# Hymba layer on one Trainium2 core: the mixer's weight splits moved into the first FFN, by way of DRAM

## The chip, the core and the metric

The kernel runs on one core of a Trainium2 chip. Times are device microseconds (us) of one execution. The engines are TensorE (PE), VectorE (DVE), ScalarE (ACT), GpSimd (POOL) and SyncE (SP), and 16 DMA engines move data between DRAM and the on-chip memory. A run's time is compared by the median of several executions; the profile is that of a further execution.

## What is computed

One decoder layer on x of 1024 tokens by D = 1024, float32, with 16 learned meta tokens put in front (T = 1040):

```python
h = h + 0.5 * swiglu(rms_norm(h), ffn1_w_in, ffn1_w_out)
u = rms_norm(h) @ w_in                      # one combined projection
o = concat(hgrn2(u[hgrn]), stick_breaking(u[sb]))
h = h + o @ w_out
h = h + 0.5 * swiglu(rms_norm(h), ffn2_w_in, ffn2_w_out)
```

The FFNs have a width of 2816. `hgrn2` is a gated linear recurrence with 4 heads of 128, `stick_breaking` an attention with 8 heads of 64, held in 4 pairs. What matters here is `w_in` (its columns 0 to 2047 are the recurrence's q, f, v and g, and 2048 and up the attention's q, k and v) and `w_out` (1024 by 1024).

## The kernel before

**Three products for one.** All float32 products are computed as three in the reduced type fp32r. A weight block w is split into a high part wh (a cast) and a low part wl = w - wh, and PE adds wh x-high, wl x-high and wh x-low. So each weight block costs one load, one cast and one subtraction before PE can use it. The FFNs do that in `operand` (cast by ACT in L277, subtraction by DVE in L279) on blocks loaded in L284. The mixer does it in `split_w` (load by SP in L141 into a tile `raw`, cast by ACT in L148, subtraction by DVE in L150), for one column of 128 outputs by 1024 inputs (`col_tile`) or one piece of `w_out` of 512 by 128.

**FFN1-in** (`fast_in`, to about 500 us) multiplies by `ffn1_w_in` in a scheme with seven products where a 2 x 2 block product has eight; a call of `quad` does one such product of 256 output columns, on weight blocks and their sums, which POOL makes in L292 from four raw blocks. The tokens are in three parts of 352, 344 and 344: the last two go through the scheme, and the first goes along as plain products (`also`). First come 3 pairs of quads without `also`, and then 8 pairs, each a gate quad and an up quad. A steady quad takes PE 21.37 us (268.46 to 289.8 in the trace), in groups of 12 matmuls. Raw blocks have 8 buffers (4 are loaded for a quad), wh and wl have 3 each. Six times in a steady quad a finished sum is taken out of PSUM by `gate` (it ends in a silu on ACT, L395, L416 or L419) or by `up` (it ends in a multiplication on DVE, L398, L424 or L428); the results go to DRAM as `act1...` by POOL's DMA queue. `between` calls `turn_x` after each quad, which turns the input x for later (L612 to L728).

**FFN1-out** (`fast_out`, about 500 to 760 us) works in steps with names; the last is A22. Its products are L592, on halved operands that ACT and DVE make in L521 and L522. In the second part of A22 the mixer's norm runs along (L210 to L211, L1454 to L1459), and at q = 5 and 7 of A22 the k and v columns of attention pair 0 (2560 and 3072) are loaded and split (`early_w`), from a pool `we`, after an eviction.

**The mixer** (about 720 to 1430 us) takes the rest of its weights from a pool `wm` with two buffers of `raw`, `wh` and `wl` each: the q column 2048 of pair 0 first, the other nine attention columns in `sb_project` within `weave`, and the 16 recurrence columns in `hgrn_fill`, one ahead of their use. The last 14 or so of these run while the attention's blocks do (`braid`, about 920 to 1210 us), between matmuls that depend on DVE and ACT (L1072, L1121 and L1208 on PE; L1187 is DVE's part of the scores and L1215 to L1223 the stick-breaking chain). Then comes the recurrence (L831 to L980) with the first half of the output projection, and the second half (`mix_out`, L1250 to L1254; eight pieces of `w_out` each from pools `wo` and `wo2`). FFN2 (from about 1390 us) has the form of FFN1.

**What sets the order.** PE's order is written out by hand (`manual_schedule` and the generators that take turns). The other engines' instructions are put in order by a scheduler, with hints such as `tc.issue_after(instruction)`. Every engine runs its own queue in order, and so does SP with the DMAs that it issues; POOL issues DMAs too. A pool's tile is given again when its last reader is done; pools that follow each other share memory, so that a new tile may have to wait for an old one of another pool.

## Time and profile before

| | |
|---|---|
| three runs | 2099.42, 2100.28, 2101.04 us (median 2100.28) |
| profiled execution | 2096.69 us, of which 2095.0 are the span from the first to the last instruction |
| granted clock of TensorE | 0.995 of full, mean |
| instructions | 32157 |
| bytes moved by DMA | 301.12 MB, mean 144 GB/s |

The profile is taken from one execution. Its page gives busy time by engine, the span in 40 slices, the DMA queues, the chain of work that ended last (followed back from the last instruction, at each step to what released it), and the costliest groups of instructions. "a<-b" after an engine and a line is the output and the inputs by the program's names; "PE x <- DVE y" in the list of waits is an idle PE that was released by DVE's y. "SPq" and "POOLq" are the queues that issue DMAs. q1 are the DMAs issued by SP, q0 those issued by POOL. The view by windows sums the busy time of each engine in a stretch of the span.

### The profile page before, as it was taken

The page shows a single profiled execution, that of the slowest core. Times are in us where ns is not written, and L with a number is a line of the kernel's source. Part 1 is how long each engine was busy: PE and PEld are TensorE (multiplying, and loading weights), DVE is VectorE, ACT ScalarE, POOL GpSimd, SP SyncE. Part 2 cuts the span into 40 slices and gives each one's busy share as a digit, 9 for nine tenths or more (in the row PEclk, how much of TensorE's full clock was granted, in tenths as well). Part 3 has the DMA queues.
Part 4 walks back from the last instruction along what each step waited for, and adds up shares of the span by engine and source line. Part 5 has one row for each costly group of instructions (what it writes and reads, how often), then busy time and mean ns, then how long its engine had stood idle before and what let it go on. Part 6 is the DMA issues. An engine that isn't in the chain of part 4 may idle for free.

```text
span 2095.0 us, 32157 instructions
## 1 busy us (share of the span) xinstructions
PE 2026.5 (97%) x11520; PEld 1830.5 (87%) x11520; DVE 1387.2 (66%) x2140; ACT 901.6 (43%) x1860; POOL 644.6 (31%) x710
## 2 busy tenths in 40 slices
PE   7999999999999999999999998998999999999998
PEld 6999999999999989988887978886788888888887
DVE  6875544545489952258878766659767676676774
ACT  8543333333465633456666514235223233234443
POOL 2475545452000002343344300112555454440000
PEclk9999999999999999999999999999999999999999
DMA  7643333325867735435454162334333233359464
GB/s 199 188 145 121 114 108 103 99 84 192 253 201 222 237 116 163 143 127 131 121 147 120 53 253 66 97 111 126 96 101 111 93 109 101 106 196 330 136 198 136
DMA packets 272566, 301.12 MB, mean 144 GB/s; under 512 B 24694, under 2 KB 199158, under 8 KB 272406
## 3 DMA queue, kind: packets, MB, share of 16 engines
q1 hardware_dynamic: 254710, 248.62, 39.0%
q0 software_dynamic: 16656, 50.44, 6.5%
q8 instruction: 91, 1.49, 0.3%
q14 instruction: 69, 0.57, 0.1%
q10 hardware_dynamic: 1040, 0.00, 0.0%
HBM read 216.42 MB, written 82.57 MB: 143 GB/s over the span
## 4 chain that ended last, share of the span: by engine, by line
PE 83%; DVE 7%; ACT 2%; issue 1%; DMA 0%; POOL 0%; SPq 0%; DVEq 0%; ACTq 0%; POOLq 0%
PE o L592 16%; PE qb L320 13%; PE qc L320 9%; PE qa L320 8%; PE qd L320 6%; PE proj L163 5%; PE proj L164 5%; PE proj L165 5%; PE o L558 4%; PE flip L1072 2%; PE lvl L841 2%; PE wo L164 1%; PE wo L163 1%; PE wo L165 1%; DVE keep L1218 1%
## 5 line engine op out<-in xcount | busy, mean ns | idle before, releaser
L320 PE MATMUL qb<-T,wh 128*128 128x344 f32 (+1 forms) x1056 | 311.7, 358 | 9.7 <-DVE u L362 5.8
L279 DVE TENSOR_TENSOR wl<-s,wh 128x512 fp32r<-128x512 f32 x176 | 202.4, 1151 | 112.7 <-ACT wh L277 110.0
L320 PEld LDWEIGHTS qb<-T,wh 128*128 128x128 f32 x1056 | 193.0, 189 | 35.2 <-ACT wh L277 7.5
L592 PE MATMUL o<-parts 128*128 128x512 f32 x924 | 209.9, 389 | 0.0
L320 PE MATMUL qa<-B,wh 128*128 128x344 f32 (+1 forms) x704 | 209.1, 361 | 0.0
L277 ACT CAST wh<-s 128x512 fp32r<-128x512 f32 x176 | 109.4, 622 | 224.6 <-PE qb L320 154.1
L163 PE MATMUL proj<-xh,wh 128*128 128x344 f32 (+2 forms) x576 | 205.5, 357 | 0.0
L592 PEld LDWEIGHTS o<-parts 128*128 128x128 f32 x924 | 173.3, 188 | 36.0
L164 PE MATMUL proj<-xh,wl 128*128 128x344 f32 (+2 forms) x576 | 199.8, 347 | 1.1 <-DVE wl L150 1.1
L165 PE MATMUL proj<-xl,wh 128*128 128x344 f32 (+2 forms) x576 | 199.0, 346 | 0.0
L279 DVE TENSOR_TENSOR wl<-raw,wh 128x512 fp32r<-128x512 f32 x172 | 153.3, 896 | 68.0 <-ACT wh L277 64.4
L277 ACT CAST wh<-raw 128x512 fp32r<-128x512 f32 x172 | 105.8, 620 | 194.7 <-PE qc L320 97.1
L320 PE MATMUL qb<-T,wl 128*128 128x344 f32 (+1 forms) x528 | 188.3, 357 | 0.0
L320 PE MATMUL qd<-X,wh 128*128 128x352 f32 x704 | 180.8, 324 | 1.2 <-DVE X L667 1.2
L592 PE MATMUL o<-t,w 128*128 128x344 f32 x924 | 148.5, 320 | 3.9 <-DVE t L522 2.2
L592 PEld LDWEIGHTS o<-t,w 128*128 128x128 f32 x924 | 145.7, 188 | 5.6 <-DVE t L522 3.3
L292 POOL TENSOR_TENSOR s<-raw 128x512 f32<-128x512 f32 x88 | 121.5, 1381 | 92.6 <-DVE wl L279 68.3
L320 PEld LDWEIGHTS qa<-B,wh 128*128 128x128 f32 x704 | 128.5, 188 | 16.0
L1218 DVE TENSOR_TENSOR_SCAN keep<-keep 128x144 f32<-128x144 f32 (+6 forms) x112 | 128.0, 1146 | 6.7 <-ACT keep L1214 4.4
L1223 POOL TENSOR_TENSOR sig<-sig,keep 128x144 f32<-128x144 f32 (+3 forms) x64 | 87.1, 1361 | 140.4 <-DVE keep L1218 91.1
L320 PE MATMUL qa<-B,wl 128*128 128x344 f32 (+1 forms) x352 | 126.0, 358 | 0.3 <-DVE wl L279 0.3
L320 PEld LDWEIGHTS qd<-X,wh 128*128 128x128 f32 x704 | 124.7, 189 | 1.4 <-DVE X L667 1.4
(331 smaller groups left out, 4530.7 us busy)
## 6 DMA issues: line engine op xcount, KB each, us to landing
raw<-in_ffn_w_in_dram SPq DMA_DIRECT2D x208, 256.0 KB, 3.1
raw<-in_ffn_w_out_dram SPq DMA_DIRECT2D x176, 256.0 KB, 4.0
raw<-in_w_in_dram SPq DMA_DIRECT2D x28, 512.0 KB, 4.2
ks<-kD SPq DMA_DIRECT2D x32, 260.0 KB, 5.2
ak<-in_ffn_w_out_dram SPq DMA_DIRECT2D x22, 256.0 KB, 5.4
v<-vD SPq DMA_DIRECT2D x8, 576.0 KB, 4.8
hT<-xD SPq DMA_DIRECT2D x8, 520.0 KB, 7.2
xD<-xts POOLq DMA_DIRECT2D x16, 256.0 KB, 2.7
```

What stands on the lines that cost most here:

```text
L163: nc.tensor.matmul(ps, wh[:, s], xs, start=k == 0, stop=False)
L164: nc.tensor.matmul(ps, wl[:, s], xs, start=False, stop=False)
L165: nc.tensor.matmul(ps, wh[:, s], xl[:, k, c0 : c0 + n], start=False, stop=k == nk - 1)
L277: nc.scalar.copy(hi, src)
L279: nc.vector.tensor_sub(lo, src, hi.bitcast(F32))
L292: op(t, x, y)
L320: nc.tensor.matmul(ps, a[:, k, :], b[:, k0 + k, :], start=start and k == 0 and i == 0, stop=k == 3 and i == 2, skip_group_check=True,)
L558: nc.tensor.matmul(ps[m], y[:, s], z, start=f == 0 and e == 0, stop=f == D_FF // P - 1 and e == 2,)
L592: nc.tensor.matmul(banks[bank][m], y[:, m * P : (m + 1) * P], z, start=start and q == 0 and e == 0, stop=q == nq - 1 and e == 2, skip_grou ...
L841: nc.tensor.matmul(ps[:, j, :], KB[:, META + c * P : META + (c + 1) * P], QA[:, c * P : (c + 1) * P], start=True, stop=True,)
L1218: nc.vector.tensor_tensor_scan(out=kv, data0=kv, data1=kv, initial=1.0 if last else keep[:, end : end + 1], op0=ALU.mult, op1=ALU.bypass,)
L1223: nc.gpsimd.tensor_mul(sig, sig, keep[:, 1 : nk + 1])
```

## The change

In FFN1-in, from the eighth quad on, each taking of a sum (`taken`) advances a generator by one block: 512 inputs by 128 outputs of a weight of the mixer. It loads the blocks in fours into 8 buffers `early`, casts a block on ACT into the first half of a tile `both` (3 buffers), subtracts on DVE into the second half, and one step later stores the tile to DRAM by SP. There are 50 blocks: the two halves of 17 columns (k, v and q of attention pair 0, and all recurrence columns but the first two) and the 16 pieces of `w_out`. For these `split_w` gets `parts`, and loads wh and wl with two DMAs, without `raw` and without work of ACT or DVE. The nine columns of the attention's other pairs and the first two recurrence columns are split as before. The loads of columns 2560 and 3072 stand at q = 1 and 3 of A22 now, with no `issue_after`. The blocks' pool `ahead` (28 KB in a partition) lies in FFN1-in's memory, and the tiles `raw` of `we`, `wo` and `wo2` are gone.

```diff
+    def split_ahead(self, pool, groups):
+        def load(views):
+            raws = []
+            for v in views:
+                t = pool.tile([P, 512], F32, tag="raw", name="early", bufs=8)
+                nc.sync.dma_start(t.rearrange("p (k f) -> p k f", k=4), v)
+                raws.append(t)
+            return raws
...
+        made = split = None
+        for block in blocks():
+            if split:
+                nc.sync.dma_start(split[0], split[1].bitcast(F32))
+            split = None
+            if made:
+                dst, src = made
+                both = pool.tile([P, 2, 512], F32R, tag="both", name="both", bufs=3)
+                nc.scalar.copy(both[:, 0], src)
+                nc.vector.tensor_sub(both[:, 1], src, both[:, 0].bitcast(F32))
+                split = dst, both
+            made = block
+            yield
...
-    def split_w(self, view):
+    def split_w(self, view, parts=None):
         nc = self.nc
         n = int(np.prod(view.shape[1:]))
+        if parts is not None:
+            got = []
+            for i, tag in enumerate(("wh", "wl")):
+                t = self.wp.tile([P, n], F32R, tag=tag, name=tag, bufs=self.w_bufs)
+                nc.sync.dma_start(t.bitcast(F32), parts[:, i])
+                got.append(t)
+            return got
...
     def col_tile(self, w, col):
-        return self.split_w(w[:, col : col + P].rearrange("(k p) f -> p k f", p=P))
+        return self.split_w(
+            w[:, col : col + P].rearrange("(k p) f -> p k f", p=P), self.parted.get(col)
+        )
...
             def gate(i, j, ps, plus):
...
+                taken(at)
...
+                        for col in [2560, 3072, 2048] + self.columns_of_heads()[2:]:
+                            t = self.parted[col] = self.dram.tile([P, 2, D], F32, name=f"win{col}")
+                            for h in range(2):
+                                pieces.append((
+                                    t[:, :, 512 * h : 512 * h + 512],
...
+                        for k0 in (4, 0):
+                            for m in range(KT):
+                                t = self.dram.tile([P, 2, 512], F32, name=f"wout{k0}{m}")
+                                self.parted[k0, m] = t
...
+                    def taken(at):
+                        if len(seen) > 6:
+                            with tc.issue_after(at.ins):
+                                next(turning[1], None)
...
-                            if q in (5, 7):
-                                col = {5: 2560, 7: 3072}[q]
-                                with tc.issue_after(self.evicted.ins):
-                                    early_w.append(self.col_tile(a["w_in"][0], col))
+                            if q in (1, 3):
+                                early_w.append(
+                                    self.col_tile(a["w_in"][0], {1: 2560, 3: 3072}[q])
+                                )
```

Compiled, PE has the same 11200 instructions in the same order, and POOL the same 715. DVE has 2156 in place of 2139, ACT 1842 in place of 1825, and SP 1076 in place of 943; these counts are of the program and hold instructions that the page's table leaves out.

More of the change, by code (lines that the diff above doesn't have):

```diff
@@ L134, in weights, with blocks @@
         self.raw_bufs, self.w_bufs, self.split_on_vector = raw, split, on_vector
-    def split_w(self, view):
+    def split_ahead(self, pool, groups):
+        nc = self.nc
+        def load(views):
[5 more added lines that the diff above has]
+            return raws
+        def blocks():
+            nxt = load(groups[0][0])
+            yield None
+            for (_, makes), after in zip(groups, groups[1:] + [((), None)]):
+                raws, nxt = nxt, load(after[0])
+                for dst, make in makes:
+                    yield dst, make(raws)
+            yield None
+            yield None
+        made = split = None
[11 more added lines that the diff above has]
+            yield
@@ new lines, in plain_groups, with quad_group, kept @@
+    def plain_groups(self, pieces):
+        return [
+            ([v for _, v in pieces[i : i + 4]],
+             [(d, lambda raws, j=j: raws[j]) for j, (d, _) in enumerate(pieces[i : i + 4])])
+            for i in range(0, len(pieces), 4)
+        ]
+    def quad_group(self, pool, w_in, col, dst):
+        nc = self.nc
+        views = [
+            w_in[512 * h : 512 * h + 512, col + P * i : col + P * i + P]
+            .rearrange("(k p) f -> p k f", p=P) for i, h in ((0, 0), (1, 0), (1, 1), (0, 1))
+        ]
+        s = {}
+        def kept(name, op, x, y):
+            t = s[name] = pool.tile([P, 512], F32, tag="sum", name="sum", bufs=3)
+            op(t, x, y)
+            return t
+        add, sub = nc.gpsimd.tensor_add, nc.gpsimd.tensor_sub
+        return views, [
+            (dst[0], lambda r: r[0]),
+            (dst[1], lambda r: r[3]),
+            (dst[4], lambda r: kept(1, add, r[1], r[2])),
+            (dst[2], lambda r: kept(2, sub, s[1], r[0])),
+            (dst[5], lambda r: r[2]),
+            (dst[3], lambda r: kept(3, sub, r[0], r[1])),
+            (dst[6], lambda r: kept(4, sub, r[3], s[2])),
+        ]
@@ L759, in project, with columns_of_heads @@
             yield 12 * n * 0.42
+    heads_plan = [(kind, h) for h in range(4) for kind in "vfqg"]
+    def columns_of_heads(self):
+        first = {"v": 1024, "f": 512, "q": 0, "g": 1536}
+        return [first[kind] + P * h for kind, h in self.heads_plan]
     def hgrn_fill(self, xh, xl, pool, dst):
         nc = self.nc
-        plan = [(kind, h) for h in range(4) for kind in "vfqg"]
-        first = {"v": 1024, "f": 512, "q": 0, "g": 1536}
+        plan, cols = self.heads_plan, self.columns_of_heads()
         def staged(n):
@@ L1409, in run @@
                     drain(steps)
-                    drain(turning[0])
+                    for x in turning:
+                        drain(x)
                 px = self.pool("xhat1", ctx=c1)
```

38 lines of the change are left out of this document (28 added, 10 removed).

## The prediction

> **What bounds the kernel now.** First the page's busy line and its chain that ended last:
>
> ```profile
> PE 2026.5 (97%) x11520; PEld 1830.5 (87%) x11520; DVE 1387.2 (66%) x2140; ACT 901.6 (43%) x1860; POOL 644.6 (31%) x710
> ...
> PE 83%; DVE 7%; ACT 2%; issue 1%; DMA 0%; POOL 0%; SPq 0%; DVEq 0%; ACTq 0%; POOLq 0%
> ```
>
> TensorE (PE) sets the time nearly everywhere; the change touches none of its instructions, so it can win only the gaps in PE and lose only by making new ones. Where the gaps are is told by the windows view, cut at the stages (columns: us, then busy us of PE, weight loads, DVE, ACT, POOL, then clock, DMA share, GB/s):
>
> ```profile
> 183.00:365.00 182.00, 182.00 (x1161) 181.84 (x1160) 89.75 (x135) 60.64 (x111) 91.32 (x98) 1.00 0.34 108
> 690.00:760.00 70.00, 66.59 (x426) 65.61 (x425) 56.51 (x123) 36.54 (x82) 6.40 (x12) 1.00 0.57 176
> 920.00:1210.00 290.00, 276.42 (x1789) 244.79 (x1788) 230.37 (x317) 181.76 (x459) 112.74 (x147) 0.99 0.41 115
> 1210.00:1330.00 120.00, 108.59 (x783) 96.60 (x782) 83.34 (x172) 37.93 (x126) 7.30 (x7) 1.00 0.43 151
> 1400.00:1520.00 120.00, 108.43 (x464) 87.02 (x463) 95.33 (x148) 49.21 (x88) 44.85 (x42) 0.96 0.35 110
> ```
>
> In FFN1-in (183 to 365) PE has no gap, and DVE, ACT and DMA are half idle or more: the new work goes there. At the end of FFN1-out (690 to 760) and in the mixer, DVE is 70 to 81% busy and PE loses 3.4, 13.6 and 11.4 us: the old work comes out of there. The waits of PE in those stretches say on whom (us in total, times, longest):
>
> ```profile
> PE o L592 <- DVE w L522: 1.7, 1, 1.7
> PE o L592 <- DVE t L522: 1.7, 1, 1.7
> ...
> PE proj L164 <- DVE wl L150: 1.1, 1, 1.1
> ...
> PE flip L1072 <- DVE wu L1187: 8.6, 16, 1.9
> PE flip L1072 <- DVE wm L1187: 2.5, 4, 1.1
> PE flip L1121 <- DVE wu L1187: 1.5, 2, 1.0
> ...
> PE flip L1072 <- DVE vm L831: 1.5, 1, 1.5
> ...
> PE wo L164 <- DVE wl L150: 1.5, 1, 1.5
> ```
>
> Only two of these (1.1 and 1.5) wait on a mixer split itself (L150). The others wait on other DVE work, which a split on the same queue may have delayed.
>
> **The change, part by part: what is removed.** The splits by line (min/median/max ns):
>
> ```profile
> L148 ACT CAST wh<-raw x44: 613/1048/1061, 714.0 to 1396.2; 128x1024 fp32r<-128x1024 f32 x28, 128x512 fp32r<-128x512 f32 x16
> L150 DVE TENSOR_TENSOR wl<-raw,wh x44: 670/1216/2858, 722.2 to 1396.9; 128x1024 fp32r<-128x1024 f32 x28, 128x512 fp32r<-128x512 f32 x16
> ```
>
> 33 of the 44 go: 17 columns of 1024 (1.05 us ACT, 1.2 us DVE each) and 16 output pieces of 512 (about 0.62 and 0.69). That is 28 us of ACT and 31 us of DVE, but it counts only where DVE is late.
>
> 1. *k and v of pair 0, end of FFN1-out.* The chain of waits runs here through DVE, and both splits lie on it:
>
> ```profile
> 713.24 3.94 DMA act<-act16T
> ...
> 722.33 1.14 DVE wl L150
> ...
> 727.66 1.14 DVE wl L150
> ```
>
> Without them the chain is 2 x 1.14 = 2.3 us shorter, out of 3.4 us of PE gaps: -2.3 (0 to -3.4). In their place four loads of 512 KB are issued about 709, ahead of that act load on SP's queue. 2 MB at the 350 GB/s derived below are 6 us; the operands behind are issued some 10 us ahead of use, so I take 0 (to +3).
>
> 2. *q of pair 0.* One wait goes, -1.1:
>
> ```profile
> 767.32 0.50 PE L164 MATMUL proj<-xh,wl 128*128 128x512 f32 x1 [1.12 <-DVE wl L150]
> 754.63 1.06 DVE L1454 SCALAR_TENSOR_TENSOR nt<-hT,gm,rs 128x344 f32<-128x344 f32 x2 [3.77 <-ACT rs L1450]
> ```
>
> The two loads now wait for tiles that the norm gives up near its last step (754.6); two of 512 KB should land some 6 us later, 6 us ahead of that matmul.
>
> 3. *14 recurrence columns, 920 to 1210.* 14 x 1.2 = 17 us leave a DVE that is busy 230 of 290, and PE waits 12.6 us on its L1187. That is 22 waits of 0.6 us each, spread over the stage, while a split falls about every 21 us; by DVE's order at most 3 or 4 of the long ones stand shortly behind one. I take -2 (0 to -5, 4 splits of 1.2).
>
> 4. *Output projection, first half (8 pieces).* One wait of 1.5 (on L831) comes directly behind a split of 0.69: -0.7 (0 to -3).
>
> 5. *Second half.* From the timeline:
>
> ```profile
> 1373.95 10.17 SPq L141 DMA_DIRECT2D raw<-in_w_out_dram  x4
> ...
> 1380.55 1.14 ACT L148 CAST wh<-raw 128x512 fp32r<-128x512 f32 x2
> 1381.73 2.00 DVE L150 TENSOR_TENSOR wl<-raw,wh 128x512 fp32r<-128x512 f32 x2
> ...
> 1383.18 0.50 PE L164 MATMUL wo<-oH,wl 128*128 128x512 f32 x1 [1.47 <-DVE wl L150]
> ```
>
> The first parts now land by themselves before 1381.7: -1.5 (nothing else is late there).
>
> 6. *FFN2's opening.* Its first raw loads were issued only here, since their tiles overlap the mixer's raw tiles:
>
> ```profile
> 1414.81 3.29 SPq L284 DMA_DIRECT2D raw<-in_ffn_w_in_dram  x6
> ...
> 1432.51 1.67 ACT L277 CAST wh<-raw 128x512 fp32r<-128x512 f32 x3
> 1433.34 1.28 DVE L279 TENSOR_TENSOR wl<-raw,wh 128x512 fp32r<-128x512 f32 x2
> ```
>
> Without raw tiles in the mixer they follow the new loads near 1390, and in the changed instruction order three operand splits stand ahead of the second half. Three DVE subtractions of 0.69 leave an opening where PE waits on DVE and ACT: up to -2.1; I take -1.5, since part of them filled a pause.
>
> Removed together: 2.3 + 1.1 + 2 + 0.7 + 1.5 + 1.5 = **9.1 us**.
>
> **What is added.** 50 blocks, six to a quad of FFN1-in, from the eighth quad on: 8.3 quads of 21.4 us (178 us, about 183 to 365). Each has a load of 256 KB, an ACT copy and a DVE subtraction of 128x512, and a store of 512 KB. Nearest rows, all in FFN1 and FFN2:
>
> ```profile
> L277 ACT CAST wh<-raw 128x512 fp32r<-128x512 f32 x172 | 105.8, 620 | 194.7 <-PE qc L320 97.1
> L279 DVE TENSOR_TENSOR wl<-raw,wh 128x512 fp32r<-128x512 f32 x172 | 153.3, 896 | 68.0 <-ACT wh L277 64.4
> ```
>
> 50 x 0.62 = 31 us bring ACT from 33% to 50% of the window; 50 x 0.69 to 0.90 = 35 to 45 us bring DVE from 49% to 69 to 74%. By sums that is hidden. What covers it is the time between an operand's making and its use:
>
> ```profile
> 278.26 0.62 ACT L277 CAST wh<-raw 128x512 fp32r<-128x512 f32 x1 [3.20 <-PE qd L320]
> 278.92 0.69 DVE L279 TENSOR_TENSOR wl<-raw,wh 128x512 fp32r<-128x512 f32 x1
> ...
> 281.85 0.32 PE L320 MATMUL qb<-T,wh 128*128 128x344 f32 x1
> ```
>
> This operand is ready at 279.61 and used at 281.85: 2.2 us to spare, enough for one copy ahead of it on ACT (0.62) and one subtraction on DVE (0.69 to 0.90), not for a wait. And there is a new wait: the copy takes one of three buffers, which is free once the store of three blocks before has landed. In the quads whose evictions are DVE's, the copies stand on ACT's queue between the casts of PE's operands, and those queue behind the waiting copy; for them DVE's subtraction, and PE, wait. So the transfers decide:
>
> ```profile
> q1 hardware_dynamic: 21090, 11.84, 20.4%
> q0 software_dynamic: 3440, 9.83, 13.5%
> ...
> vD<-vhl SPq DMA_DIRECT2D x8, 512.0 KB, 4.7
> ...
> 500.00:550.00 50.00, 49.86 (x312) 49.57 (x312) 23.91 (x39) 19.57 (x36) 6.32 (x9) 1.00 0.91 319
> ```
>
> The first two are 200 to 400 us: loads 11.84 MB in 20.4% of 200 us, 290 GB/s; stores 9.83 MB in 13.5%, 364 GB/s. The last row moves 319 GB/s at a share of 0.91, 350 at full share. A quad adds 6 x 0.262 MB of loads (5.4 us at 290) and 6 x 0.524 MB of stores (8.6 us at 364) to 0.34 x 21.4 = 7.3 us: **21.3 us of 21.4**. The DMA engines are just full. The nearest store of that size lands 4.7 us after its issue (vD). Followed by hand through a quad with such copies, operands then keep some 2 us; at twice that landing, PE would lose 1 to 3 us in each of four such quads. I take +2.5, near the lower end, since the demand still fits; ends 0 and +20 (demand 10% higher, 8.3 quads). The mixer's weights now weigh twice the bytes, at shares of 0.41 to 0.57: 0.
>
> Two pages of the Trainium skill bear on this place. HBM Reference (Specifications) has a lone core's stream well above 358 GB/s, at about 425. No row here reaches it (350 above); by it a quad's 7.0 MB would take an estimated 16.5 us, the term would be 0 and the sum -9.1. SBUF: State Buffer (SBUF: two separate sides) speaks against the change: a DVE instruction with two SBUF inputs and a GpSimd one that reads SBUF lock each other out for a whole instruction. The trace agrees as far as the subtraction's 896 ns mean beside 0.69 undisturbed goes; by it POOL's operand sums would come up to 0.69 us later for each new subtraction, which the ends above hold.
>
> **Sum.** -9.1 + 2.5 = -6.6. The profiled execution took 2096.69 us (span 2095.0), so 2090.1 on its scale; the median of the runs, 2100.28, lies 3.6 higher, so 2093.7: **2094 us**.
>
> **The rivals.**
>
> *A, slower: the transfers are over-full in FFN1-in.* Loads in 512 B rows mixed with as many stores may be served worse than either alone. The page's slices of 52 us:
>
> ```profile
> GB/s 199 188 145 121 114 108 103 99 84 192 253 201 222 237 116 163 143 127 131 121 147 120 53 253 66 97 111 126 96 101 111 93 109 101 106 196 330 136 198 136
> ```
>
> None moves more than 330 GB/s, and a quad (108 GB/s now, 2.3 MB, plus 4.7 MB) would ask for 328. For it: that row; the casts queued behind waiting copies. Against it: a full share leaves raw loads two quads of lookahead, and stores ran at 364. Each quad then lasts as its DMA demand; at 8% over, 1.8 us x 8.3 = 15, net +5.9: 2106. It turns the sign from 9.1 / 8.3 = 1.1 us a quad, a demand 5% over.
>
> *B, no change: the relief does not reach PE.* In the mixer, waits on L1187 are chains through PE, ACT and DVE, which stay as long with a freer DVE. Parts 3, 4 and 6 give 0: -2.3 - 1.1 - 1.5 + 2.5 = -2.4: 2098. For it: most waits are 0.6 us long with no split in front.
>
> *C, the loads come late.* A column was one load, split far ahead; now two loads of 512 KB wait until PE frees the tiles, in SP's order:
>
> ```profile
> raw<-in_w_in_dram SPq DMA_DIRECT2D x28, 512.0 KB, 4.2
> ```
>
> Two in a row need 4.2 to 8.4 us. In the recurrence a column lasts 21 us, so this can bite only at 709 to 766. Two late by 4.2 cost 8: net +1.8: 2102.
>
> *D, better: all hidden.* Term 0, part 3 at -4, 4 at -1.5, 6 at -2: -12.4: 2088.
>
> That the blocks are not done by then is no case of its own: 15 quads are left for the 8.3.
>
> **How the numbers follow.** The forecast has 0.42 (-4.3 to -11), D 0.08, A 0.27, B 0.15, C 0.08. A measurement of this kernel tells about 0.2% (4.2 us) from no change. Faster by more than that: forecast and D, 0.50. Within: B, half of C and 0.04 of A, 0.23. Slower: the rest of A and C, 0.27. For 8 in 10 the range goes from D's time to A at a demand 10% over (+20 - 9.1 = +10.9, 2111): 2088 to 2110. The likeliest case alone: 2089 to 2096.
>
> **What would show it.** Right: PE stays at 182 of 182 in 183 to 365, with a DMA share near 1.0; the gaps at 766 and 1383 are gone; PE gains about 2 us each in 690 to 760 and 920 to 1210 and about 1.5 in 1400 to 1520. Wrong by A: waits of PE on ACT wh L277 or DVE wl L279 before 365, idle ACT ahead of the copies put down to stores. Wrong by B: the waits on L1187 stay at 12.6. Wrong by C: PE waits on loads at L163 or L164. A start of FFN1-out later than now would also show a loss that no term here holds: transfers displaced at the start of the blocks.

## The result and the profile after

The changed kernel is slower: 2104.64 us (median of 19 runs, 2097.98 to 2112.16) against 2097.85 for the kernel before (19 runs, 2094.61 to 2101.04). The ratio is 1.0032, with a 95% interval of 1.0025 to 1.0040. The profiled execution took 2105.35 us, of which 2103.6 are the span; its kernel before had 2096.69 and 2095.0. The time lies inside the stated range, but the direction was forecast wrongly.

The page of the changed kernel, first its busy line, then the chain that ended last, then DMA traffic in 40 slices:

```profile
PE 2031.5 (97%) x11520; PEld 1833.3 (87%) x11520; DVE 1403.3 (67%) x2157; ACT 905.9 (43%) x1877; POOL 644.2 (31%) x710
...
GB/s 198 161 161 126 320 326 291 205 99 122 292 203 212 266 127 173 128 163 129 167 158 137 120 267 56 122 204 85 96 100 110 90 110 101 105 196 326 134 199 135
...
PE 71%; DVE 6%; DMA 3%; issue 1%; ACT 1%; SPq 0%; DVEq 0%; ACTq 0%
```

DMA has come into the chain (3%, 0% before), and the fifth to seventh slices, FFN1-in with the blocks, move 291 to 326 GB/s in place of 103 to 114. The stages by windows, cut as before:

```profile
183.00:365.00 182.00, 176.53 (x1102) 174.02 (x1101) 126.56 (x172) 77.63 (x144) 88.44 (x92) 0.99 0.85 285
690.00:760.00 70.00, 67.75 (x432) 67.18 (x431) 63.09 (x130) 39.81 (x86) 6.43 (x12) 1.00 0.69 224
920.00:1210.00 290.00, 281.19 (x1839) 251.29 (x1838) 214.91 (x303) 174.34 (x450) 112.98 (x152) 1.00 0.52 148
1210.00:1330.00 120.00, 108.31 (x771) 95.48 (x770) 78.65 (x165) 35.83 (x120) 7.10 (x7) 1.00 0.44 157
1400.00:1520.00 120.00, 107.91 (x459) 87.01 (x458) 95.01 (x147) 49.27 (x88) 40.92 (x41) 0.94 0.35 111
```

PE now has gaps in FFN1-in (176.5 of 182) and fewer in the recurrence columns' stage (281.2 of 290 busy, 276.4 before). The waits of PE in the changed kernel, in the stretches 0 to 150, 150 to 500, 700 to 780, 920 to 1230 and 1340 to 1420:

```profile
PE qc L400 <- ACT wh L357: 3.7, 1, 3.7
...
PE qb L400 <- DVE u L442: 5.7, 6, 1.8
PE qd L400 <- DVE sp L478: 1.2, 2, 0.8
...
PE spread L279 <- DVE diag L276: 1.6, 1, 1.6
...
PE flip L1159 <- DVE wu L1274: 5.0, 13, 0.9
PE flip L1159 <- DVE wm L1274: 2.5, 4, 1.1
PE flip L1208 <- DVE wu L1274: 1.0, 1, 1.0
...
PE wo L243 <- DVE hT L1340: 1.1, 1, 1.1
PE wo L244 <- DMA wl<-wout: 0.5, 1, 0.5
```

Of the 5.7 us on L442, 1.5 are an old wait: it stood at 143.7 before and stands at 150.1 now, just past the cut at 150. New in FFN1-in are 4.2 and, on L478, 1.2 us.

The lines of the program have moved by some 80: L400 is the FFN's matmul (L320 before), L357 and L359 the operand's cast and subtraction (L277, L279), L442 and L478 evictions by DVE, L372 POOL's weight sums (L292), L525 its sums of activations, L168 and L169 the blocks' copy and subtraction.

**Where the time went.** PE runs the same 11520 matmuls in the same order in both traces, so the start of each can be compared with the start of the same one before. The lag of the changed kernel (us), by the time in the trace before:

| stretch | lag at its end | change in it | the prediction's term |
|---|---|---|---|
| 0 to 76 | -0.3 | -0.3 | |
| 76 to 183, start of the blocks' loads | 6.4 | **+6.7** | none |
| 183 to 400, FFN1-in with blocks | 15.6 | **+9.2** | +2.5 |
| 400 to 690 | 15.8 | +0.2 | |
| 690 to 760, part 1 | 14.2 | -1.6 | -2.3 |
| 760 to 920, part 2 | 13.5 | -0.7 | -1.1 |
| 920 to 1210, part 3 | 7.7 | **-5.8** | -2 |
| 1210 to 1382, part 4 | 6.4 | -1.3 | -0.7 |
| 1382 to 1395, part 5 | 5.4 | -1.0 | -1.5 |
| 1395 to 1520, part 6 | 7.6 | **+2.2** | -1.5 |
| 1520 to the end | 8.4 | +0.8 | |

Parts 1 to 6 sum to -8.2, where -9.1 was forecast. FFN1 cost 15.9 where 2.5 was forecast.

**The start.** The timeline of the changed kernel near 80 us:

```profile
80.45 4.96 SPq L146 DMA_DIRECT2D early<-in_w_in_dram  x5
...
86.14 0.62 ACT L168 CAST both<-early 128x512 fp32r<-128x512 f32 x1 [7.14 <-DMA early<-in_w_in_dram]
...
86.67 0.61 ACT L357 CAST wh<-s 128x512 fp32r<-128x512 f32 x1
87.19 1.14 ACT L168 CAST both<-early 128x512 fp32r<-128x512 f32 x2
...
87.33 0.66 PE L400 MATMUL qc<-T,wh 128*128 128x344 f32 x1 [3.65 <-ACT wh L357]
```

The first three copies (L168) belong to the eighth quad, 100 us later, but stand here in ACT's queue, in front of an operand's cast. ACT idles 7.14 us for a load that SP has just issued; then PE waits 3.65 us. The wait has a tail; the windows right behind it (the clock is the number after the five engines):

```profile
84.00:86.00 2.00, 0.00 (x0) 0.00 (x0) 0.00 (x0) 0.00 (x0) 0.00 (x0) 0.93 1.15 325
86.00:88.00 2.00, 0.66 (x1) 0.29 (x1) 0.69 (x1) 1.86 (x4) 0.00 (x0) 0.50 1.14 343
88.00:90.00 2.00, 1.94 (x7) 1.94 (x8) 0.79 (x3) 1.71 (x4) 1.29 (x1) 0.50 1.13 338
90.00:92.00 2.00, 2.00 (x9) 2.00 (x8) 1.38 (x3) 0.38 (x1) 0.92 (x1) 0.50 0.95 280
```

PE is busy but its clock is at 0.50 for some 6 us, in which the lag grows by 2 more.

**FFN1-in.** Its longest wait in full (timeline of the changed kernel):

```profile
321.94 2.15 SPq L163 DMA_DIRECT2D win<-both  x2
...
328.45 0.62 ACT L168 CAST both<-early 128x512 fp32r<-128x512 f32 x1 [3.21 <-issue]
...
328.98 0.62 ACT L357 CAST wh<-s 128x512 fp32r<-128x512 f32 x1
...
329.62 0.69 DVE L359 TENSOR_TENSOR wl<-s,wh 128x512 fp32r<-128x512 f32 x1 [5.08 <-ACT wh L357]
...
332.77 1.36 DVE L169 TENSOR_TENSOR both<-early,both 128x512 fp32r<-128x512 f32 x1
...
333.66 1.61 POOL L372 TENSOR_TENSOR s<-s,raw 128x512 f32<-128x512 f32 x1
...
334.49 1.34 DVE L169 TENSOR_TENSOR both<-early,both 128x512 fp32r<-128x512 f32 x1
...
336.35 0.50 DVE L442 TENSOR_TENSOR u<-qb,p 128x344 f32<-128x344 f32 x1
...
337.00 0.40 PE L400 MATMUL qb<-T,wh 128*128 128x344 f32 x1 [1.79 <-DVE u L442]
```

PE waits for an eviction by DVE (L442), which is late behind other work of DVE, two subtractions of blocks among it. That work came late itself. DVE stood idle 5.08 us for the cast of an operand, which stood in ACT's queue behind the copy of a block, and that copy had waited 3.21 us. The profile names no releaser there ("issue"), but the copy needs the buffer of `both` of three blocks before, whose store was issued at 321.94 and took 6.4 us to land, to 328.38. With the lower clock behind it (338 to 342, shown in the last section) the lag grows here from 10.5 to 14.0, by 3.6 of the 9.2 us. This is the new wait that the prediction describes. What the stage's loss comes from in sum, the experiments below ask.

### The profile page after: what moved, and what is told of

Read it like the earlier page. It is cut to its first block, busy times and chain, and to the rows that moved or that the text cites. A ratio compares the mean times of both kernels' runs of the same rounds, so it can differ in the third digit from the quotient of the medians.

```text
span 2103.6 us, 32391 instructions
## 1 busy us (share of the span) xinstructions
PE 2031.5 (97%) x11520; PEld 1833.3 (87%) x11520; DVE 1403.3 (67%) x2157; ACT 905.9 (43%) x1877; POOL 644.2 (31%) x710
## 4 chain that ended last, share of the span: by engine, by line
PE 71%; DVE 6%; DMA 3%; issue 1%; ACT 1%; SPq 0%; DVEq 0%; ACTq 0%
PE o L674 14%; PE qb L400 10%; PE qc L400 7%; PE qa L400 7%; PE proj L244 4%; PE proj L243 4%; PE proj L245 4%; PE o L640 4%; PE qd L400 3%; PE flip L1159 2%; PE lvl L928 2%; DVE keep L1305 1%; PE wo L243 1%; PE wo L244 1%; PE wo L245 1%
## 5 line engine op out<-in xcount | busy, mean ns | idle before, releaser
L400 PE MATMUL qb<-T,wh 128*128 128x344 f32 (+1 forms) x1056 | 312.8, 359 | 14.5 <-DVE u L442 14.4
L359 DVE TENSOR_TENSOR wl<-s,wh 128x512 fp32r<-128x512 f32 x176 | 199.0, 1131 | 109.6 <-ACT wh L357 106.9
L400 PEld LDWEIGHTS qb<-T,wh 128*128 128x128 f32 x1056 | 193.8, 190 | 41.6 <-ACT wh L357 9.1
L400 PE MATMUL qa<-B,wh 128*128 128x344 f32 (+1 forms) x704 | 209.4, 361 | 0.2 <-ACT p L437 0.2
L357 ACT CAST wh<-s 128x512 fp32r<-128x512 f32 x176 | 109.8, 624 | 205.8 <-PE qb L400 147.5
L400 PE MATMUL qb<-T,wl 128*128 128x344 f32 (+1 forms) x528 | 188.6, 357 | 0.0
L359 DVE TENSOR_TENSOR wl<-raw,wh 128x512 fp32r<-128x512 f32 x172 | 159.1, 929 | 43.1 <-ACT wh L357 38.9
L400 PE MATMUL qd<-X,wh 128*128 128x352 f32 x704 | 182.0, 326 | 2.1 <-DVE sp L478 1.2
L357 ACT CAST wh<-raw 128x512 fp32r<-128x512 f32 x172 | 106.4, 622 | 169.7 <-PE qc L400 93.5
L372 POOL TENSOR_TENSOR s<-raw 128x512 f32<-128x512 f32 x88 | 125.5, 1427 | 94.2 <-DVE wl L359 69.0
L400 PEld LDWEIGHTS qa<-B,wh 128*128 128x128 f32 x704 | 128.5, 188 | 16.7 <-ACT p L437 0.6
L1305 DVE TENSOR_TENSOR_SCAN keep<-keep 128x144 f32<-128x144 f32 (+6 forms) x112 | 132.4, 1183 | 12.6 <-ACT keep L1301 8.0
L400 PEld LDWEIGHTS qd<-X,wh 128*128 128x128 f32 x704 | 125.9, 191 | 3.0 <-DVE sp L478 1.7
L400 PE MATMUL qa<-B,wl 128*128 128x344 f32 (+1 forms) x352 | 126.0, 358 | 0.7 <-DVE wl L359 0.7
```

The costliest lines, as they stand in the source:

```text
L357: nc.scalar.copy(hi, src)
L359: nc.vector.tensor_sub(lo, src, hi.bitcast(F32))
L372: op(t, x, y)
L400: nc.tensor.matmul(ps, a[:, k, :], b[:, k0 + k, :], start=start and k == 0 and i == 0, stop=k == 3 and i == 2, skip_group_check=True,)
L1305: nc.vector.tensor_tensor_scan(out=kv, data0=kv, data1=kv, initial=1.0 if last else keep[:, end : end + 1], op0=ALU.mult, op1=ALU.bypass,)
```

## The experiments

All lags are against the trace before, by the same matmuls; medians are beside runs of the kernel before on the same chip. A lag belongs to one profiled execution, which took more than its kernel's median in e2 (by 4.7 us), e18 (3.5) and e8 (3.2), less in e5 (3.0) and e13 (2.4), and was within 1.5 us of it in the others. So differences of a few us between two kernels' lags are hints, and the medians decide.

| kernel | median us (before) | ratio, interval | lag at 183 | gained lag 183 to 400 | lag 760 | 1210 | 1395 | 1520 | end |
|---|---|---|---|---|---|---|---|---|---|
| changed | 2104.64 (2097.85) | 1.0032, 1.0025 to 1.0040 | 6.4 | 9.2 | 14.2 | 7.7 | 5.4 | 7.6 | 8.4 |
| e1_start8 | 2095.35 (2098.12) | 0.9990, 0.9981 to 0.9999 | 0.3 | 3.5 | 1.7 | -5.4 | -6.8 | -3.1 | -3.0 |
| e2_start8_ring6 | 2094.27 (2098.12) | 0.9980, 0.9970 to 0.9989 | 0.1 | 6.1 | 6.3 | -0.8 | -1.7 | 0.8 | 1.6 |
| e3_work_no_store | 2098.79 (2098.12) | 1.0007, 0.9998 to 1.0016 | 0.3 | 0.7 | 1.1 | -0.6 | 1.1 | 1.0 | 1.0 |
| e4_move_no_split | 2125.82 (2098.12) | 1.0133, 1.0119 to 1.0147 | 5.6 | 19.8 | 26.7 | 24.8 | 26.4 | 26.5 | 27.0 |
| e5_relief_only | 2092.02 (2097.53) | 0.9971, 0.9959 to 0.9982 | 0.0 | 0.0 | -2.4 | -9.6 | -12.8 | -10.0 | -8.4 |
| e8_no_dve_sub | 2097.56 (2097.53) | 1.0000, 0.9991 to 1.0009 | -1.2 | 6.2 | 8.4 | 1.5 | -1.0 | 1.1 | 2.7 |
| e9_late4 | 2091.97 (2097.53) | 0.9976, 0.9966 to 0.9985 | 0.3 | 0.9 | 0.2 | -6.4 | -9.6 | -6.0 | -5.0 |
| e10_early4 | 2094.08 (2097.53) | 0.9984, 0.9975 to 0.9993 | -0.4 | 3.1 | 2.5 | -4.5 | -5.5 | -3.6 | -3.3 |
| e11_late4_ffn2_held | 2090.66 (2097.82) | 0.9960, 0.9947 to 0.9973 | 1.6 | 1.1 | 1.5 | -5.1 | -7.8 | -6.2 | -6.3 |
| e12_late4_ffn2_kv47 | 2088.74 (2097.82) | 0.9958, 0.9946 to 0.9970 | -0.8 | 0.0 | -2.3 | -9.3 | -10.6 | -10.7 | -9.3 |
| e13_pinned | 2099.81 (2097.82) | 1.0009, 1.0001 to 1.0018 | -0.1 | 9.8 | 8.2 | 1.2 | -1.5 | 0.2 | 0.5 |
| e14_start8_t4 | 2090.36 (2097.82) | 0.9966, 0.9953 to 0.9979 | -1.0 | 2.4 | -0.4 | -7.0 | -9.3 | -7.5 | -7.6 |
| e15_quad7 | 2095.80 (2098.33) | 0.9978, 0.9969 to 0.9987 | 0.9 | 4.3 | 3.0 | -4.0 | -5.0 | -2.3 | -1.0 |
| e16_quad10_pinned | 2099.15 (2098.33) | 1.0008, 0.9999 to 1.0017 | -0.9 | 8.4 | 7.2 | -0.1 | -2.1 | 1.2 | 1.1 |
| e17_best_t4 | 2086.20 (2098.33) | 0.9942, 0.9930 to 0.9955 | -2.5 | 0.0 | -4.7 | -11.5 | -12.4 | -12.0 | -11.9 |
| e18_before_t4 | 2095.56 (2098.53) | 0.9987, 0.9978 to 0.9996 | -0.8 | 0.0 | 1.3 | 1.1 | 2.4 | 2.3 | 2.4 |

### The start: e1_start8

```diff
-                        if len(seen) > 6:
+                        if len(seen) > 7:
```

> The changed kernel with one number changed: the blocks begin at the ninth quad of FFN1-in (len(seen) > 7), a gate quad, in place of the eighth, an up quad. In the trace of the changed kernel three ACT copies of the first blocks stand near 80 us, and PE loses 3.65 us there and then runs about 5 us at a clock of 0.50 (6 us in all). Theory (queue): these copies stood free in ACT's queue because an up quad's takings hold DVE's instructions only, and they waited for their loads with the operands' casts behind them. Then the 6 us go: about 2098.5 in place of 2104.6. Rival (loads): the 2 MB of first loads, which stay at about 80 us here, delay the raw blocks of the quads; then the wait stays and the time is 2104 to 2105.

2095.35. The copies stand in the ninth quad now and the lag at 183 is 0.3 in place of 6.4. The first loads still come near 80 us, so it was the copies' place in ACT's queue. More went than that: 3.5 us are lost in FFN1-in, not 9.2.

### What costs in FFN1-in: the ring, the work, the transfers

e2_start8_ring6, on e1:

```diff
-    name="both", bufs=3)
+    name="both", bufs=6)
```

> As the kernel that begins at the ninth quad, with 6 buffers in place of 3 for the split blocks (both). PE loses 9.3 us between 217 and 361 us in the changed kernel, in waits on evictions by DVE. Theory (ring): ACT's copies wait for a store to give a buffer back (15 us of idle ACT in the trace), and the casts of PE's operands stand behind them, then DVE's subtractions, then its evictions; with 6 buffers the stores have twice as long, and the 9.3 fall below 3: about 2092. Rival (transfers): the DMA engines are over-full (share 0.96 to 1.03 in the up quads) and raw blocks come late however many buffers there are: 7 to 9 stay, about 2098.

2094.27, neither the 2092 of the one theory nor the 2098 of the other; the intervals of e1 and e2 overlap. ACT's idle time ahead of a copy for a store fell (put down to `win` stores: 23.5 us in e1, 9.2 here). The trace loses 6.1 us, more than e1's 3.5, but this execution took 4.7 us more than its median. So the ring is not shown to be the main cause of e1's loss, and what part of it it has stays open.

e3_work_no_store, on e1, with the mixer's splits as before:

```diff
-            if split:
-                nc.sync.dma_start(split[0], split[1].bitcast(F32))
             split = None
```

> Begins at the ninth quad; loads the 50 blocks and splits them on ACT and DVE, but stores nothing; the mixer splits its weights itself as in the kernel before, and loads k and v of pair 0 where that did. So only the loads and the work of ACT and DVE are left in FFN1-in. Ring and transfers both expect no loss there without the stores: 2098 to 2099, as before. Rival (work): 50 copies and 50 subtractions more bring DVE to 69% and that alone makes the evictions late: about 2105 to 2107.

2098.79: no loss beyond the error, 0.7 us in the trace, with all 50 copies and subtractions there. The stage by windows in e3, and below it (its own fence) in the changed kernel:

```profile
226.00:400.00 174.00, 173.54 (x1105) 172.90 (x1104) 130.56 (x177) 82.89 (x155) 88.74 (x93) 1.00 0.57 172
```

```profile
205.00:378.00 173.00, 167.53 (x1046) 165.02 (x1045) 123.93 (x168) 78.96 (x147) 83.64 (x88) 0.99 0.92 307
```

DVE and ACT are as busy in e3, but DMA's share is 0.57 in place of 0.92. The work alone is hidden, as the sum in the prediction had it. DVE's subtractions meet POOL's sums here too (between 226 and 400, 40 that overlap with one took 1.34 us, 72 others 0.69). So it needs the stores for a loss, at least with the start in the ninth quad.

e4_move_no_split, on e1, with the mixer's splits as before:

```diff
-                nc.sync.dma_start(split[0], split[1].bitcast(F32))
+                for i in range(2):
+                    nc.sync.dma_start(split[0][:, i], split[1])
...
-                both = pool.tile([P, 2, 512], F32R, tag="both", name="both", bufs=3)
-                nc.scalar.copy(both[:, 0], src)
-                nc.vector.tensor_sub(both[:, 1], src, both[:, 0].bitcast(F32))
-                split = dst, both
+                nc.scalar.copy(src[:, :8], src[:, :8])
+                nc.vector.tensor_copy(src[:, :8], src[:, :8])
+                split = dst, src
```

> Begins at the ninth quad; the same bytes in and out, but no splits: each block's tile is stored twice (256 KB each), after a copy of 8 columns on ACT and on DVE that keeps its place; a tile comes back by the ring of 8 loads, so neither engine waits for a store before a copy. The mixer splits its weights itself as in the kernel before. Transfers: the loss in FFN1-in is there without the work, 6 us or more: 2104 or more. Ring: the transfers alone cost 0 to 2: 2098 to 2100.

2125.82, which the transfers' theory has by number (2104 or more) but not by reason. Here a load must wait for the two stores of its tile, and ACT and DVE wait for the loads; the waits around the tile `early` in e4 (us, times):

```profile
  DMA early<-in_w_in_dram: 35.8, 14
  ACT early L168: 30.4, 13
  DMA early<-in_w_out_dram: 15.1, 6
```

The edit made a wait of its own that the changed kernel doesn't have (51 us of idle engines for loads). It shows how dear an in-order queue behind a late transfer is, and tells nothing of the dispute.

e8_no_dve_sub, on e1:

```diff
-                nc.vector.tensor_sub(both[:, 1], src, both[:, 0].bitcast(F32))
+                nc.scalar.copy(both[:, 1], src)
```

> As the kernel that begins at the ninth quad (2095.4; its trace loses 3.5 us in FFN1-in), but the low half of each block is a second copy by ACT in place of DVE's subtraction, so it is no split. Theory (port): DVE's subtractions meet POOL's sums (their mean is 1.40 us where POOL runs, 0.69 where it doesn't) and make DVE's evictions late; without them the loss goes, in spite of ACT's extra 31 us: about 2092. Rival (transfers): full DMA engines are enough, and with ACT fuller the loss is the same or larger: 2095 or more.

2097.56. The stage in e8, and below it (its own fence) in e1:

```profile
205.00:378.00 173.00, 167.72 (x1063) 166.56 (x1062) 81.50 (x123) 102.46 (x193) 82.79 (x90) 1.00 0.92 306
```

```profile
205.00:378.00 173.00, 170.71 (x1083) 169.80 (x1082) 127.27 (x172) 78.88 (x149) 83.93 (x93) 1.00 0.91 301
```

DVE has a third less to do than in e1 (81.5 in place of 127.3), ACT has more (102.5 in place of 78.9), DMA's share is nearly the same, and nothing is won: PE loses more in the trace, and the median equals that of the kernel before. ACT's added copies could hide a gain, so e8 alone doesn't rule the collisions out. With e3, which has them all and loses nothing beyond the error, the port theory falls as the main cause.

e14_start8_t4, on e1:

```diff
-                    self.t_bufs, self.in_bufs = 2, 8
+                    self.t_bufs, self.in_bufs = 4, 8
```

> As the kernel that begins at the ninth quad (2095.4, 3.5 us lost in FFN1-in), with 4 buffers in place of 2 for POOL's sums of activations (t, L525). In that trace POOL's queue waits for the stores of act1..T, which land after 4.7 us in place of 2.3, and POOL's weight sums stand behind. Theory (stores hold POOL): with 4 buffers that wait is gone, and with it most of the loss: about 2092. Rival: raw blocks and the rest of the transfers are late anyway, or DVE is late by its collisions with POOL: 2094 to 2096.

2090.36, 5 us less than e1. What it removes is seen in the timeline of e1, where POOL's sum of activations waits for a store, and POOL's weight sums start behind it at 299.80:

```profile
297.61 0.93 POOL L525 TENSOR_TENSOR t<-sg,t 128x344 f32<-128x344 f32 x1 [1.84 <-DMA act15T<-t]
...
299.80 1.29 POOL L372 TENSOR_TENSOR s<-raw,s 128x512 f32<-128x512 f32 x1
...
305.62 0.39 PE L400 MATMUL qb<-T,wh 128*128 128x344 f32 x1 [1.06 <-DVE u L442]
```

But in the trace 2.5 us are won at 113 and 142 us, ahead of the blocks, the loss of FFN1-in fell only from 3.5 to 2.4, and 2.2 us more than in e1 are won behind 400, where the edit changes nothing. e18_before_t4 (this edit alone on the kernel before) measures that part:

> The kernel before with nothing changed but 4 buffers in place of 2 for POOL's sums t in FFN1-in. In the traces with 4 of them, two waits of 1.5 us at about 113 and 142 us (ahead of the blocks) shrink to 0.3. If that gain has nothing to do with the split weights, it is here too: 2.5 us, about 2095.5. Rival: it comes only with the change's other order, and this is as before, 2098.

2095.56, ratio 0.9987 (0.9978 to 0.9996): 3 us belong to these buffers alone, as expected; its trace, too, wins 2.4 us between 76 and 183.

### How many blocks, and where: e9, e10, e13, e15, e16

e9_late4 and e10_early4 take a block at four of a quad's six takings (the position in the quad is `p`):

```diff
-                        if len(seen) > 6:
+                        if len(seen) > 7 and p > 1:     # e9_late4
+                        if len(seen) > 7 and p < 4:     # e10_early4
```

> Begins at the ninth quad; a block at four takings of a quad in place of six, the third to the sixth, so 13 quads of 14 in place of 8.3. The demand on the DMA engines falls from 21.3 to 16.7 us of 21.4. The first two takings, which are left out, are where POOL's three sums of a quad run. Both theories expect a gain; port: nothing is lost in FFN1-in, about 2092; transfers: the same, and the same time as the next kernel.

> As the one before, with the same rate, at the first to the fourth taking of a quad, so that the first two blocks of each quad fall on POOL's sums. Port: 2 to 3 us are lost in FFN1-in all the same, about 2094 to 2095. Transfers: as the one before, about 2092.

2091.97 and 2094.08; losses of 0.9 and 3.1 us in FFN1-in, at DMA shares of 0.72 and 0.73 (205 to 378). With a third less traffic per quad the loss nearly goes where the first two takings are left out. The place matters in the traces at equal rate; the two intervals overlap, so that the times alone don't part them. Both numbers are what the port theory forecast; the transfers' theory had 2092 for both and misses the second by 2 us. Since e3 and e8 speak against it as the main cause, either the collisions cost only beside late transfers, or the place acts in another way; no run parts these two.

e13_pinned is the changed kernel with ACT's copies held in their quad; e15_quad7 begins the blocks at the seventh quad (a gate quad); e16_quad10_pinned is e13 with the start at the tenth (an up quad):

```diff
-                            with tc.issue_after(at.ins):
+                            with tc.issue_after(at.ins), tc.issue_after(self.last_p1.ins):   # e13, e16
-                        if len(seen) > 6:
+                        if len(seen) > 5:     # e15
+                        if len(seen) > 8:     # e16
```

> The changed kernel, blocks from the eighth quad on as there, with one hint more: each taking's instructions on ACT also stand behind the same quad's first ACT copy out of PSUM (L437), so that in an up quad ACT's copies have a place too. Queue: the three early copies near 80 us were only a matter of their place; the 6 us there go, and the loss in FFN1-in falls to that of the start at the ninth quad (3.5): about 2095. Rival: the eighth quad itself is too early, and of the 9.3 us lost in FFN1-in most stays: 2099 or more.

> The changed kernel with the blocks from the seventh quad on, a gate quad. Phase: what counts is in which quad of a pair the blocks begin, since the loads come in fours and a pair has twelve takings; then this loses about 3.5 us in FFN1-in, as the start at the ninth quad does: about 2095. Early: the earlier the start, the more is lost: 9 us or more, 2100 or more.

> As the kernel with ACT's copies held (2099.8, start at the eighth quad, 9.8 us lost in FFN1-in), with the start at the tenth quad, an up quad again. Phase: 8 to 10 us are lost as there: about 2100. Early: less than 4 are lost: 2095 or less.

2099.81, 2095.80 and 2099.15. e13 has no start wait (lag -0.1 at 183) and loses 9.8 us all the same, as its rival had it. Starts in a gate quad (seventh, ninth) lose 4.3 and 3.5, starts in an up quad (eighth, tenth) 9.8 and 8.4, and the medians go the same way: the place in the pair decides, not the earliness. (No gate start was run with the copies held; the changed kernel, an up start without the hint, loses 9.2.)

By which step that shift of six takings acts was not tried and stays open. The mean DMA share doesn't tell: it is 0.91 in e1 and e13, 0.92 in e15 and the changed kernel. ACT's longest wait ahead of a block's copy goes along with the loss: 4.4, 4.5 and 5.1 us in the three up starts (changed, e13, e16), 2.7 and 3.0 in the two gate starts. But e2 and e8 lose 6 us in their traces with no such wait above 3.1, so it isn't all.

### The relief: e5_relief_only, e11, e12, e17

e5_relief_only, on e1: only three blocks are split, and every entry of `parted` is one of two tiles.

```diff
-                            t = self.parted[col] = self.dram.tile([P, 2, D], F32, name=f"win{col}")
-                            for h in range(2):
+                            if col == 2560:
+                                t = self.dram.tile([P, 2, D], F32, name=f"win{col}")
+                            self.parted[col] = t
+                            for h in range(2) if col == 2560 else ():
...
```

> Only three blocks are split in FFN1-in (column 2560 and one piece of the output projection, from the ninth quad on); every other ready-made column or piece of the mixer loads these same two, so that its weights are not the reference's but its loads are of the same number and size. So this has the mixer's relief without the cost in FFN1-in. In the traces, the changed kernel wins 7.2 us from the end of FFN1-in to the end, and the one that begins at the ninth quad 6.6. Theory: the relief is that much and independent of FFN1-in: about 2091 to 2092, where before is 2098. Rival (displaced loads): part of the relief comes with the order in which FFN2's and FFN1-out's first loads fall, which the 50 blocks push about: 2088 or less, or 2095 or more.

2092.02, ratio 0.9971 (0.9959 to 0.9982): a relief of 5.5 us in the medians, as expected, and of 8.4 in the trace. By 1395 the trace has won 12.8, and by 1520 it has given 2.8 back, which points at FFN2's opening. There the changed kernel's timeline has:

```profile
1395.66 11.28 SPq L364 DMA_DIRECT2D raw<-in_ffn_w_in_dram  x9
...
1402.54 0.62 ACT L357 CAST wh<-raw 128x512 fp32r<-128x512 f32 x1 [1.63 <-DMA raw<-in_ffn_w_in_dram]
...
1404.66 0.69 DVE L359 TENSOR_TENSOR wl<-raw,wh 128x512 fp32r<-128x512 f32 x1 [0.78 <-ACT wh L357]
...
1405.27 0.68 DVE L1340 TENSOR_TENSOR hT<-wo,hT 128x512 f32<-128x512 f32 x1
...
1406.01 0.50 PE L243 MATMUL wo<-oH,wh 128*128 128x512 f32 x1 [1.06 <-DVE hT L1340]
```

FFN2's first splits wait for raw blocks that SP issues behind 16 loads of parts, and the output projection's evictions (L1340) stand behind them. e11_late4_ffn2_held, on e9, holds them back:

```diff
+                with tc.issue_after(self.last_rms.ins):
-                next(steps)
+                    next(steps)
```

> As the kernel with four late takings (2092.0), and FFN2's first weight casts on ACT are held behind the last ACT step of the norm (L263), where they stood before the change. In its trace the three moved splits stand ahead of the last evictions of the output projection, wait for raw blocks that are loaded behind 16 loads of parts, and PE loses 1.95 us and about 2 more at a lower clock. Theory: these 4 us come back: about 2088. Rival: DVE bounds the opening, and the three subtractions cost there what they cost here: 2090 to 2092.

2090.66 against 2091.97 for e9 (intervals overlap), inside the rival's range. The wait of 1.95 us is gone from the trace, and between 1395 and 1520 it gives back 1.6 where e9 gave 3.6: half of the 4 us expected. That DVE bounds the opening, as the rival says, would explain the rest; no run shows it.

e12_late4_ffn2_kv47, on e11:

```diff
-                            if q in (1, 3):
+                            if q in (4, 7):
-                                    self.col_tile(a["w_in"][0], {1: 2560, 3: 3072}[q])
+                                    self.col_tile(a["w_in"][0], {4: 2560, 7: 3072}[q])
```

> As the one before, with the four loads of k and v of pair 0 (2 MB) at q = 4 and 7 of the last step of FFN1-out in place of 1 and 3. In the traces PE waits 1 to 2 us there at a spread of the norm, which stands behind halved operands whose loads came late behind these 2 MB. Theory: spread out, they cost no wait: 1 to 2 us less than the one before, about 2087. Rival: now k or v come late for their first products: 2 us or more slower than the one before.

2088.74. The wait at the norm's spread is not in its trace; a wait of 1.83 on a halved operand stands in its place, and 690 to 760 gains 2.2 as in e11 (2.3). The medians' 1.9 us are inside the intervals; its trace also lost nothing in FFN1-in. So this move is not shown to help. e17_best_t4 is e12 with 4 buffers for t:

> Four late takings a quad, FFN2's casts held, k and v at q = 4 and 7 (2088.7), and 4 buffers for POOL's sums t. If those buffers help beside fewer takings as they do beside six, the last 0 to 1 us of FFN1-in goes: 2088. Rival: with 16.7 us of transfers in 21.4 nothing is left to win there: the same, 2088.7.

2086.20, ratio 0.9942 (0.9930 to 0.9955), the fastest kernel here, 11.9 us under the kernel before in the trace and 12.1 in the medians; by e18, 3 of them are the buffers'. FFN1-in in e17:

```profile
205.00:378.00 173.00, 173.00 (x1103) 172.82 (x1103) 117.62 (x158) 73.53 (x135) 88.18 (x96) 1.00 0.75 239
```

PE has no gap, with the same blocks as the changed kernel spread over more quads, at a share of 0.75. In the trace of e12, without the added buffers, it has none either, at 0.73.

## Why the prediction was wrong

**The step that failed is the cost in FFN1-in:** "I take +2.5, near the lower end, since the demand still fits". It measured 9.2: 5.4 us of new waits of PE, about 1.6 at a lower clock behind the longest of them, and about 2 that no listed wait holds. The demand of 21.3 us in 21.4 was near the truth: 0.92 of the window was used, up quads alone 0.96 to 1.03. But a mean that just fits doesn't hide a transfer when engines wait for it in order. Raw blocks landed in 5.0 us where 3.0 were usual, stores of blocks in 5.2, and single ones in 6.4. The prediction had the path (a copy that waits for a store, an operand's cast behind it, DVE and PE behind that), and the wait at 337 shows it; what it had wrong is the size, which it took from the fit of the means.

Nor is the size a matter of the share alone. At 0.90 to 0.93 of DMA time six kernels beside the changed one (e1, e2, e8, e13, e14, e15) lost 2.4 to 9.8 us in their traces, and at 0.72 to 0.75 five (e9 to e12 and e17) lost 0 to 3.1; much of the difference goes with where in the pair and in the quad the blocks stood (e13, e15, e16; e9, e10). What is shown is that the work without stores costs nothing beyond the error (e3) and that the whole, spread over more quads, can be hidden (e17). By which queue the lateness reaches PE is known in part: the ring in the wait at 337, POOL's sums behind late stores of activations in e1 (e14, 1 of 3.5 us, where the traces vary by more). How the 9.2 us divide is open.

Rival A named the over-full transfers, with a condition (5% over) that wasn't needed, and of its signs one came: idle ACT ahead of the copies, put down to stores (20 us), while PE's waits were on evictions (L442, L478) and not on operands. That its 2106 lies near 2104.6 is luck: 6.7 us of the loss are the start, which it doesn't hold.

**A step was missing: the start, 6.7 us.** The prediction treated the blocks as beginning at the eighth quad and named displaced transfers only among what could make it wrong. ACT's queue has the first three copies 100 us ahead of that. The loads displaced nothing (e1 has them too); the wait was the copies' (e1, e13).

**The removed splits were right in sum, in part by luck:** -8.2 against -9.1. Part 3 won 3.8 us more than forecast and part 6 lost 3.7 more, and the two cancel.

- Part 3 was worth more (-5.8, beyond the end of -5 that it was given): PE's waits on the scores' DVE work fell from 12.6 to 8.5, and another 1.5 us came at 1154, where before PE's clock had fallen (to 0.50) behind the longest of those waits. So rival B is out.
- Part 1 (-1.6): both waits of 1.7 are gone; a new one of 1.59 at the norm's spread came in their place. This is not rival C: the loads of k, v and q came in time, and no wait on them is listed at 700 to 780. It is the "0 (to +3)" of part 1: the halved operands there waited for transfers behind the 2 MB:

```profile
736.68 0.63 ACT L603 CAST w<-raw 128x512 fp32r<-128x512 f32 x1 [1.81 <-DMA raw<-in_ffn_w_out_dram]
...
742.39 0.60 PE L279 MATMUL spread<-diag,ones_d 128*128 128x128 f32 x3 [1.59 <-DVE diag L276]
```

- Parts 2, 4 and 5 held within 0.6 us.
- Part 6 has the wrong sign (+2.2 for -1.5). The moved splits did leave the opening, but wait for loads ahead of the projection's evictions; held back, they give about half of it back (e11, in the trace).

Of the Trainium skill's two rules that the prediction weighed, the first would have set the term to 0 with a stream of about 425 GB/s (HBM Reference, Specifications); over 205 to 378 us the trace moved 307 GB/s at a share of 0.92, 334 at full share, so that stream was not reached here. The second (SBUF — State Buffer, SBUF: two separate sides) is borne out as a behaviour: in e1, 38 DVE subtractions beside POOL's work took 1.40 us and 73 others 0.69. As a price it is not shown: e3 has as many collisions and lost nothing beyond the error.

## What to carry to other kernels

Work moved into an idle-looking stage is paid for by the fullest resource of its fullest stretch, and transfers need room as engines do: here the blocks cost 2.4 to 9.8 us at 0.90 to 0.93 of DMA time, in good part by where they began, and 0 to 3.1 at 0.72 to 0.75. A demand that just fits is no ground for a cost near 0: look also at how late a single transfer can land and at the slack of the work that stands behind it in an in-order queue (at 337, a landing of 6.4 us and some 2 us of slack). Look up where the first instructions of moved work stand in each in-order queue, not only where the program asks for them; three copies whose loads were not there cost 6.7 us, most of the relief of 8.2. If the gain is real but the cost eats it, spread the work and measure the relief by itself first.

## What the runs showed of the hardware

PE's clock fell behind some waits, and not only behind long ones. In the changed kernel 3.65 us idle were followed by about 6 us at 0.50, and a wait of 1.79 at 337 by windows at 0.58 and 0.57, while a wait of 1.30 at 361 was followed by 1.00:

```profile
336.00:338.00 2.00, 1.00 (x6) 1.03 (x7) 1.97 (x5) 0.00 (x0) 0.77 (x2) 1.00 1.07 399
338.00:340.00 2.00, 2.00 (x10) 2.00 (x9) 2.00 (x3) 1.14 (x2) 1.33 (x2) 0.58 1.02 339
340.00:342.00 2.00, 2.00 (x9) 2.00 (x9) 1.95 (x4) 0.00 (x0) 0.37 (x2) 0.57 1.07 382
...
362.00:364.00 2.00, 2.00 (x15) 2.00 (x14) 2.00 (x3) 0.98 (x2) 1.31 (x2) 1.00 1.01 354
```

So was one of 1.59 at 742, and before the change the two waits of 1.7 at 733 and 737. The Trainium skill (TensorE: Matmul & The Clock Gate, Part 1: The HAM clock gate) has half the clock after an idle window of about 3.4 us; the first agrees, the dip behind 1.79 us of wait does not follow from that rule, and no run here settles what else it takes. In the two places the tail added about 2.7 and 1.6 us to waits of 3.65 and 1.79, which an estimate by wait times alone leaves out.

The changed kernel's time also varied more: 14 us between the fastest and the slowest of 19 runs, 6.4 for the kernel before. That full DMA is the reason isn't shown; e1, at a share of 0.91, varied by 4.7 us in 11 runs.
